# Token operands of an up projection stored tile by tile instead of row by row: one change to a hybrid decoder step

## The chip, the cores and the metric

The kernel runs on one core of one Trainium2 chip. The metric is the device time of one execution, in microseconds (us). Before the change it was 2911.22 us, the median of three runs (2903.2 to 2924.93).

## The reference

One layer of a hybrid decoder is computed, in float32, for a prompt of 2064 tokens (16 learned ones ahead of 2048) and for 8 short sequences of 4 new tokens each: 2096 token rows of width 1024. Attention and a state-space model make an output that is added to the rows. What the change touches is the last part, the feed-forward network:

```
xn2 = rmsnorm(x, norm2)
a, c = xn2 @ w_gate, xn2 @ w_up          # 1024 -> 2816 each
conv = conv_b + sum(conv_w[j] * ap[:, j:j+T] for j in range(3))   # ap: history and a
x = x + (gelu(conv) * c) @ w_down
```

## The kernel before

**Precision.** A float32 product is made of three TensorE products. Each operand is split into a rounded part and a rest: ScalarE (ACT) writes the rounded part, VectorE (DVE) the rest (`split`, lines 67 to 69). `mm3` then issues high by high, high by low and low by high (lines 80 to 82). One split is thus a pair of instructions, one on ACT and one on DVE.

**The up projection** is done by seven products in place of eight (a scheme of Strassen's kind, in Winograd's form). The tokens stand in three blocks of 6, 6 and 5 tiles of 128 rows (`BLOCKS`). In each block, even tiles make one half of the token columns and odd tiles the other, so a block is 3, 3 and 2.2 tiles wide (384, 384 and 280 columns, `width_of`). Each product takes one token operand of 512 features (4 groups `k` of 128) by those columns, and one weight operand. The seven token operands are sums and differences of the quarters of the normed rows. They are made once in `out_norm` (lines 1225 to 1255), in the stage that adds the attention's output projection to the rows: there ACT evicts transposed rows, POOL (GpSimd) forms the differences, and ACT's queue writes each operand to a DRAM scratch array `XB` (helper `keep`, line 1242). `XB` has, for each block, partition and operand, 4 rows (`k`) of 384 columns, so a tile of 128 columns goes out as 4 runs of 512 bytes for each partition and operand.

**Stages in order of time.** Until 1180 us: projections, state-space model, and attention over the prompt, with the output projection of the first six tiles inside it. From about 1200 to 1335 us: `out_attention(range(6, 16), ahead=True)`, the output projection, norm and `XB` writes of ten tiles, with parts of the short sequences' attention (`sample_attention`: gathers of cached keys by indirect DMA, transposes and products on TensorE) put between. From about 1335 to 2425 us: the up projection, 66 units (3 blocks, 11 pairs of feature tiles, gate and up) of 7 products of 12 matmuls, the rest of the short sequences' attention between them. Then the down projection.

**Loads of token operands.** `load_tokens` (lines 1284 to 1299) reads one operand of one block: two loads (`k` 0 and 1, then 2 and 3), each into a raw buffer, each followed by one split of 768 columns a partition (560 in the last block). It is called seven times in `up_setup` for the first block. For each later block it is called right after the last product that used the operand's old contents (`cur["turn"]` in `product`, line 1387): the *turn* of a block, at about 1740 to 1800 us and 2150 to 2195 us. Raw buffers come from pools shared with other work of the stage (tags `raw`, `A`, `z`). The SP queue issues these loads and the weight loads (`load_up`, line 1308) in one order, so a load that waits for its buffer holds up what is behind it.

**Order.** Each engine works through its instructions in a fixed order. The order is made when the program is built, by a planner that simulates a timeline with its own costs (`schedule_with_timeline_sim=True`). ACT's evictions of PSUM (line 1411) and weight splits stand in the same queue as the token splits.

Of the kernel before, what the change touches and what calls it, by code (L numbers as in the profile page):

```python
# [10 lines left out]
F32 = mybir.dt.float32  # L11
# [9 lines left out]
P = 128  # L21
# [25 lines left out]
BLOCKS = [(0, 6), (6, 12), (12, NT)]  # L47
# [3 lines left out]
def width_of(blk):  # L51

    t0, t1 = BLOCKS[blk]
    return (min(t1 * P, T) - t0 * P) // 2


def rows_of(t):
    return P if t < NT - 1 else T - P * (NT - 1)


class Step:
# [81 lines left out]
    def scratch(self, dp):  # L143
        self.KST = dp.tile([H, 2, P, TP], F32, name="KST")
        self.QST = dp.tile([2, H, 2, 64, TP], F32, name="QST")
        self.VST = dp.tile([TP, H * P], F32, name="VST")
        self.VNS = dp.tile([NS * TS, H * P], F32, name="VNS")
        self.UT = dp.tile([512, CH, NU], F32, name="UT")
        self.XNT = dp.tile([12, P, KT, P], F32, name="XNT")
        self.OT = dp.tile([H, P, T], F32, name="OT")  # L150
        self.RR = dp.tile([H, RRW], F32, name="RR")
        self.TBL = dp.tile([2, G, NST, NJ], F32, name="TBL")
        self.GT = dp.tile([CH, 512, NC], F32, name="GT")
        self.ST = dp.tile([2, 4, P, T], F32, name="ST")
        self.X1 = dp.tile([T, D], F32, name="X1")
        self.XB = dp.tile([len(BLOCKS), P, 7, 4, 3 * P], F32, name="XB")
        self.MT = dp.tile([2, P, 11, T], F32, name="MT")

    def load_x(self, xt, t):
# [1065 lines left out]
    def out_norm(self, t, xt, wp, pp):  # L1225
        nc, gp = self.nc, self.nc.gpsimd
        n = rows_of(t)
        xs = self.normed(wp, xt, n, self.g2)
        blk = min(t // 6, 2)
        at = (t - BLOCKS[blk][0]) // 2 * P  # L1230
        last = t == NT - 1
        m = n // 2 if last else P
        if t % 2 == 0:
            self.quarters = [wp.tile([P, 2, 4, P], F32, name="x" + s, tag="x" + s) for s in ("ev", "od")]
        ev, od = self.quarters
        for b in range(2):
            tp = self.half_T(pp, xs, n, b)
            for z, x in enumerate((ev, od)) if last else ((0, (ev, od)[t % 2]),):
                nc.scalar.activation(x[:, b, :, :m], tp[:, :, z * m : z * m + m], AF.Copy)

        def keep(op, x, o=1):
            nc.scalar.dma_start(out=self.XB[blk, :, op : op + o, :, at : at + m], in_=x)

        if t % 2 == 0:
            keep(0, ev[:, :, :, :m], 2)
        if t % 2 or last:
            t1 = wp.tile([P, 2, 4, P], F32, name="xt1", tag="xs")
            keep(2, od[:, 1:2, :, :m])
            gp.tensor_tensor(out=t1[:, 0, :, :m], in0=od[:, 0, :, :m], in1=ev[:, 0, :, :m], op=ALU.subtract)
            gp.tensor_tensor(out=t1[:, 1, :, :m], in0=od[:, 1, :, :m], in1=t1[:, 0, :, :m], op=ALU.subtract)  # L1250
            keep(3, t1[:, :, :, :m], 2)
            gp.tensor_tensor(out=od[:, 0, :, :m], in0=od[:, 1, :, :m], in1=od[:, 0, :, :m], op=ALU.subtract)
            keep(5, od[:, 0:1, :, :m])
            gp.tensor_tensor(out=ev[:, 1, :, :m], in0=ev[:, 1, :, :m], in1=t1[:, 1, :, :m], op=ALU.subtract)
            keep(6, ev[:, 1:2, :, :m])
# [28 lines left out]
    def load_tokens(self, blk, z):  # L1284

        L = width_of(blk)
        op = self.PLACE[z]
        x = self.fx.tile([P, 2, 4, 3 * P], F32R, name="xb", tag=f"xb{op}")
        for k in (0, 2):
            if blk and k == 0:  # L1290
                raw = self.fr.tile([P, 4, 256], F32, name="xraw", tag="raw", bufs=4).rearrange("p k f -> p (k f)")
            else:

                tag = "A" if blk or k else "z"
                raw = self.fz.tile([P, 6 * P + 2 * (tag == "A")], F32, name="xraw", tag=tag, bufs=2)
            raw = raw[:, : 6 * P].rearrange("p (k c) -> p k c", k=2)
            self.nc.sync.dma_start(out=raw[:, :, :L], in_=self.XB[blk, :, op, k : k + 2, :L])
            self.split(x[:, 0, k : k + 2, :L], x[:, 1, k : k + 2, :L], raw[:, :, :L])
        self.xs[z] = x

    def load_up(self, unit):
# [471 lines left out]
```

## Time and profile before

| What | us |
|---|---|
| median of three runs | 2911.22 |
| the profiled execution | 2908.08 |
| its span in the profile | 2906.2 |
| PE (TensorE) busy | 2729.4 |
| DVE busy | 2217.5 |
| ACT busy | 1421.6 |
| POOL busy | 977.4 |

The profile shows one execution. Busy times count instructions of an engine, and the rest of the span is idle time of that engine. Matmul ends are modelled, so a busy PE isn't PE at its peak. Idle time is put down to the instruction or DMA that ended it. The granted clock is the mean share of TensorE's full speed in a stretch, and the DMA share is the mean busy share of the core's 16 DMA engines.

### The profile page before, as it was taken

To read this page: it belongs to the slowest core of one execution; us is meant where nothing else is said; L and a number is where in the kernel's file an instruction comes from. 1 tells how busy PE (TensorE), PEld (TensorE's weight loads), DVE (VectorE), ACT (ScalarE), POOL (GpSimd) and SP (SyncE) were. 2 spreads that over 40 slices of the span, in tenths; PEclk is the share of its full clock that TensorE was granted. 3 is DMA by queue.
4 is the path that set the end of the run, shared out by engine and by line. 5 is a ranking of instruction groups with operands and counts; after the bars stand their busy time and mean duration, and the time that the engine had idled before them with its cause. 6 is when DMAs were issued, how large, how long until landed. Compare 5 with 4: busy or idle time off the path is not lost. (4 is left out here: it accounts for less than half of the span.)

```text
span 2906.2 us, 43491 instructions
## 1 busy us (share of the span) xinstructions
PE 2729.4 (94%) x14872; PEld 2353.4 (81%) x14872; DVE 2217.5 (76%) x4318; ACT 1421.6 (49%) x2887; POOL 977.4 (34%) x1381
## 2 busy tenths in 40 slices
PE   6899889989999999788999999999999999999899
PEld 6866667877887778667998998988998998777776
DVE  6648877767778899558898788888889995674565
ACT  5423334555556666336566556665565663222233
POOL 2525442114444666554243333353213441000000
PEclk9899999999999999989999999999999999999999
DMA  6675676887765342687455546455454447775562
GB/s 180 179 185 142 169 196 178 210 234 202 218 187 157 112 122 85 178 266 233 150 169 180 167 144 211 149 173 161 140 180 133 130 122 270 248 235 186 172 209 87
DMA packets 438135, 512.13 MB, mean 176 GB/s; under 512 B 91338, under 2 KB 339034, under 8 KB 436889
## 3 DMA queue, kind: packets, MB, share of 16 engines
q1 hardware_dynamic: 344440, 361.87, 42.9%
q10 hardware_dynamic: 74576, 79.09, 8.1%
q0 software_dynamic: 18896, 68.39, 7.5%
q8 instruction: 117, 1.92, 0.3%
q14 instruction: 106, 0.86, 0.1%
HBM read 381.32 MB, written 126.74 MB: 175 GB/s over the span
## 5 line engine op out<-in xcount | busy, mean ns | idle before, releaser
L80 PE MATMUL g<-xb,uw 128*128 128x384 f32 (+1 forms) x1848 | 596.0, 325 | 10.5 <-ACT uw L68 4.1
L81 PE MATMUL g<-xb,uw 128*128 128x384 f32 (+1 forms) x1848 | 595.1, 323 | 1.1 <-DVE xb L69 1.1
L82 PE MATMUL g<-xb,uw 128*128 128x384 f32 (+1 forms) x1848 | 583.5, 323 | 0.9 <-DVE uw L69 0.9
L80 PEld LDWEIGHTS g<-xb,uw 128*128 128x128 f32 x1848 | 347.5, 188 | 23.3 <-ACT uw L68 5.2
L81 PEld LDWEIGHTS g<-xb,uw 128*128 128x128 f32 x1848 | 347.9, 188 | 8.9 <-issue 2.3
L82 PEld LDWEIGHTS g<-xb,uw 128*128 128x128 f32 x1848 | 344.8, 188 | 7.9 <-DVE uw L69 1.8
L491 ACT ACTIVATE p<-S,nms 128x484 f32<-128x484 f32 (+11 forms) x360 | 210.5, 592 | 144.3 <-DVE nms L490 125.0
L69 DVE TENSOR_TENSOR uw<-uraw,uw 128x512 fp32r<-128x512 f32 x330 | 241.7, 739 | 25.3 <-ACT uw L68 23.5
L68 ACT ACTIVATE uw<-uraw 128x512 fp32r<-128x512 f32 x330 | 200.4, 625 | 113.8 <-PE g L82 70.5
L80 PE MATMUL pq<-dw,da 128*128 128x512 f32 x528 | 208.3, 396 | 15.0 <-DVE dO L1601 8.4
L490 DVE TENSOR_REDUCE nms<-S 128x1 f32<-128x484 f32 (+11 forms) x360 | 190.2, 554 | 31.8 <-PE S L485 23.1
L81 PE MATMUL pq<-dw,da 128*128 128x512 f32 x528 | 207.9, 394 | 0.0
L82 PE MATMUL pq<-dw,da 128*128 128x512 f32 x528 | 200.5, 394 | 3.1 <-DVE da L69 3.1
L80 PE MATMUL pj<-wh,x 128*128 128x512 f32 (+1 forms) x408 | 169.1, 417 | 14.9 <-DVE wk L337 5.9
L95 POOL TENSOR_TENSOR rs_y<-rs_v,half 128x8 f32<-128x8 f32 (+4 forms) x77 | 95.6, 1247 | 252.7 <-DVE rs_v L90 230.8
L68 ACT ACTIVATE da<-dt 128x1024 fp32r<-128x1024 f32 (+1 forms) x68 | 71.0, 1046 | 210.8 <-PE pq L82 133.0
L81 PE MATMUL pj<-wl,x 128*128 128x512 f32 (+1 forms) x408 | 168.7, 413 | 3.5 <-DVE wl L75 3.5
L1323 POOL TENSOR_TENSOR uraw<-uraw 128x512 f32<-128x512 f32 x66 | 111.0, 1682 | 171.0 <-DVE s L1321 124.4
L82 PE MATMUL pj<-wh,x 128*128 128x512 f32 (+1 forms) x408 | 167.6, 412 | 0.0
L484 PE MATMUL S<-kt,qs 128*128 128x484 f32 (+11 forms) x360 | 144.9, 405 | 13.6 <-ACT p L491 7.3
L521 POOL TENSOR_TENSOR p<-p,g 128x412 f32<-128x412 f32 (+13 forms) x164 | 155.7, 977 | 3.7
L553 PE MATMUL O<-wT,vt 128*128 128x256 f32 x576 | 143.6, 386 | 8.9 <-DVE wT L550 7.4
(432 smaller groups left out, 6930.4 us busy)
## 6 DMA issues: line engine op xcount, KB each, us to landing
dt<-MT SPq DMA_DIRECT2D x99, 512.0 KB
uraw<-in_w_gate_dram SPq DMA_DIRECT2D x66, 512.0 KB
uraw<-in_w_up_dram SPq DMA_DIRECT2D x66, 512.0 KB
raw<-in_w_in_dram SPq DMA_DIRECT2D x80, 256.0 KB
MT<-z ACTq DMA_DIRECT2D x44, 384.0 KB
qs<-QST SPq DMA_DIRECT2D x128, 128.0 KB
draw<-in_w_down_dram SPq DMA_DIRECT2D x55, 256.0 KB
dT<-in_w_down_dram SPq DMA_DIRECT2D x55, 256.0 KB
```

The costliest lines, as they stand in the source:

```text
L68: nc.scalar.activation(hi, src, AF.Copy)
L69: nc.vector.tensor_tensor(out=lo, in0=src, in1=hi.bitcast(F32), op=ALU.subtract)
L80: mm(out, lhsT=lh, rhs=rh, start=start, stop=False, skip_group_check=goes_on)
L81: mm(out, lhsT=lh, rhs=rl, start=False, stop=False, skip_group_check=goes_on)
L82: mm(out, lhsT=ll, rhs=rh, start=False, stop=stop, skip_group_check=goes_on)
L95: nc.gpsimd.tensor_tensor(out=y, in0=v, in1=e, op=ALU.pow)
L484: nc.tensor.matmul(dst, lhsT=qs[:, 0, c, qa : qa + M], rhs=kt[c][:, x:y], start=True, stop=False)
L490: nc.vector.tensor_reduce(out=nms[:M, z : z + 1], in_=dst, axis=AX.X, op=ALU.max, negate=True)
L491: nc.scalar.activation(p[:M, Z + x : Z + y], dst, AF.Exp, bias=nms[:M, z : z + 1], accum_out=sms[:M, z : z + 1])
L521: nc.gpsimd.tensor_tensor(out=pw[1][:M, x], in0=pw[1][:M, x], in1=g[:M, z : z + 1].to_broadcast([M, x.stop - x.start]), op=ALU.mult)
L553: nc.tensor.matmul(O[:, :N], lhsT=v, rhs=tw[:, m - a, :N], start=(m == 0), stop=(m == nb))
L1323: gp.tensor_tensor(out=a21, in0=a11, in1=a21, op=ALU.subtract)
```

## The change

`XB` is laid out as block, partition, operand, then column tile, then `k`, then 128 columns. One tile of one operand is then 2 KB in one piece for each partition. Writes of the last tile, which is 24 columns wide in each half, are issued operand by operand. A load takes two pieces of a tile and a half (3 KB a partition each) where the columns are full. In the last block, the second piece is one load of 1 KB a partition and one of 4 runs of 24 columns. Each piece is split by two pairs of instructions: tile 0 whole (512 columns) and `k` 0 and 1 of tile 1 (256), then `k` 2 and 3 of tile 1 (256) and tile 2 whole (512, in the last block 96).

```diff
-        self.XB = dp.tile([len(BLOCKS), P, 7, 4, 3 * P], F32, name="XB")
+        self.XB = dp.tile([len(BLOCKS), P, 7, 3, 4, P], F32, name="XB")
...
-        at = (t - BLOCKS[blk][0]) // 2 * P
+        at = (t - BLOCKS[blk][0]) // 2
...
         def keep(op, x, o=1):
-            nc.scalar.dma_start(out=self.XB[blk, :, op : op + o, :, at : at + m], in_=x)
+
+            for z in range(o) if last else [slice(0, o)]:
+                to = self.XB[blk, :, op + z, at, :, :m] if last else self.XB[blk, :, op : op + o, at]
+                nc.scalar.dma_start(out=to, in_=x[:, z])
...
-        for k in (0, 2):
-            if blk and k == 0:
+        kept = self.XB[blk, :, op].rearrange("p j k c -> p (j k c)")
+        n = L - 2 * P
+        for half in range(2):
+            if blk and half == 0:
                 raw = self.fr.tile([P, 4, 256], F32, name="xraw", tag="raw", bufs=4).rearrange("p k f -> p (k f)")
             else:
-                tag = "A" if blk or k else "z"
+                tag = "A" if blk or half else "z"
                 raw = self.fz.tile([P, 6 * P + 2 * (tag == "A")], F32, name="xraw", tag=tag, bufs=2)
-            raw = raw[:, : 6 * P].rearrange("p (k c) -> p k c", k=2)
-            self.nc.sync.dma_start(out=raw[:, :, :L], in_=self.XB[blk, :, op, k : k + 2, :L])
-            self.split(x[:, 0, k : k + 2, :L], x[:, 1, k : k + 2, :L], raw[:, :, :L])
+            a = 6 * P * half
+            if half == 0 or n == P:
+                self.nc.sync.dma_start(out=raw[:, : 6 * P], in_=kept[:, a : a + 6 * P])
+            else:
+                self.nc.sync.dma_start(out=raw[:, : 2 * P], in_=kept[:, a : a + 2 * P])
+                self.nc.sync.dma_start(out=raw[:, 2 * P : 6 * P].rearrange("p (k c) -> p k c", c=P)[:, :, :n],
+                                       in_=self.XB[blk, :, op, 2, :, :n])
+            for j, k0, k1, at in ((1, 2, 4, 0), (2, 0, 4, 2 * P)) if half else ((0, 0, 4, 0), (1, 0, 2, 4 * P)):
+                w = n if j == 2 else P
+                src = raw[:, at : at + (k1 - k0) * P].rearrange("p (k c) -> p k c", c=P)[:, :, :w]
+                self.split(x[:, 0, k0:k1, j * P : j * P + w], x[:, 1, k0:k1, j * P : j * P + w], src)
```

## Rows read from the trace of the kernel before

**Rows 1.** The page: the span, and the engines' busy time, share and instructions.

```profile
span 2906.2 us, 43491 instructions
...
PE 2729.4 (94%) x14872; PEld 2353.4 (81%) x14872; DVE 2217.5 (76%) x4318; ACT 1421.6 (49%) x2887; POOL 977.4 (34%) x1381
```

**Rows 2.** Windows: stretch, length, busy us by engine, clock, DMA share, GB/s.

```profile
1220.00:1260.00 40.00, 35.74 (x174) 29.64 (x174) 22.64 (x42) 14.78 (x28) 23.99 (x21) 0.91 0.91 268
1260.00:1300.00 40.00, 34.41 (x173) 29.11 (x174) 21.70 (x36) 14.81 (x28) 25.45 (x23) 0.91 0.87 275
1300.00:1340.00 40.00, 27.61 (x135) 21.79 (x134) 26.09 (x40) 18.88 (x33) 17.12 (x17) 0.87 0.87 277
...
1460.00:1760.00 300.00, 299.93 (x1690) 272.81 (x1689) 249.60 (x367) 174.20 (x290) 111.55 (x119) 1.00 0.52 161
1760.00:1800.00 40.00, 37.33 (x216) 34.84 (x214) 33.78 (x49) 25.57 (x43) 8.03 (x9) 1.00 0.80 264
...
2160.00:2200.00 40.00, 35.19 (x221) 33.79 (x219) 34.30 (x56) 23.21 (x42) 7.07 (x11) 0.96 0.55 166
...
2240.00:2420.00 180.00, 179.39 (x1393) 177.99 (x1392) 173.96 (x375) 110.88 (x218) 74.16 (x100) 1.00 0.41 122
```

**Rows 3.** What PE waited for, 1180 to 1345 us: total us, times, longest.

```profile
PE tp L188 <- DVE xs L180: 11.1, 4, 4.8
PE tps L648 <- DMA kv<-in_cache_k_dram,idx: 10.5, 6, 3.2
PE tpr L580 <- DVE rs_y L99: 5.9, 1, 5.9
...
PE Sp L654 <- DVE kT L69: 0.5, 2, 0.2
```

**Rows 4.** ACT's DMA queue, 1173 to 1186 us: packets, MB, share of 16 engines.

```profile
q10 hardware_dynamic: 2624, 1.31, 36.1%
```

**Rows 5.** The same queue, 1380 to 1460 us.

```profile
q10 hardware_dynamic: 576, 1.57, 4.9%
```

**Rows 6.** The same queue, 2100 to 2112 us.

```profile
q10 hardware_dynamic: 3722, 0.47, 28.8%
```

**Rows 7.** Splits on ACT by tile, whole span: ns min/median/max, first and last start, forms.

```profile
L68 ACT ACTIVATE uw<-uraw x330: 609/624/661, 1334.1 to 2416.8; 128x512 fp32r<-128x512 f32 x165
...
L68 ACT ACTIVATE xb<-xraw x42: 657/833/856, 1328.5 to 2193.2; 128x768 fp32r<-128x768 f32 x28, 128x560 fp32r<-128x560 f32 x14
...
L68 ACT ACTIVATE gh<-gT x32: 401/406/488, 499.7 to 610.2; 128x256 fp32r<-128x256 f32 x28, 128x336 fp32r<-128x336 f32 x4
```

**Rows 8.** Splits on DVE by tile, whole span, the same columns.

```profile
L69 DVE TENSOR_TENSOR uw<-uraw,uw x330: 670/682/2175, 1335.7 to 2418.4; 128x512 fp32r<-128x512 f32 x165
...
L69 DVE TENSOR_TENSOR xb<-xraw,xb x42: 728/946/1829, 1329.4 to 2193.9; 128x768 fp32r<-128x768 f32 x28, 128x560 fp32r<-128x560 f32 x14
...
L69 DVE TENSOR_TENSOR gl<-gT,gh x32: 405/420/509, 500.2 to 612.0; 128x256 fp32r<-128x256 f32 x28, 128x336 fp32r<-128x336 f32 x4
```

**Rows 9.** What PE waited for, 1735 to 1840 us, the first turn.

```profile
PE g L80 <- ACT c L1411: 2.0, 2, 1.3
PE g L80 <- DVE A L1420: 1.2, 1, 1.2
```

**Rows 10.** ACT in order, 1779 to 1785 us: start, us, instruction, idle before and releaser.

```profile
1781.19 0.84 ACT L68 ACTIVATE xb<-xraw 128x768 fp32r<-128x768 f32 x1 [4.94 <-DMA xraw<-XB]
1781.94 0.47 ACT L1411 ACTIVATE c<-g 128x384 f32<-128x384 f32 x1
```

**Rows 11.** What PE waited for, 2145 to 2250 us, the second turn.

```profile
PE g L80 <- ACT uw L68: 4.1, 3, 2.9
```

**Rows 12.** What PE waited for, 1325 to 1400 us, the first block's start.

```profile
PE g L81 <- DVE xb L69: 1.1, 1, 1.1
...
PE g L80 <- ACT xb L68: 0.6, 1, 0.6
```

**Rows 13.** SP's issues of token loads, whole span: ns min/median/max, first and last start.

```profile
L1297 SPq DMA_DIRECT2D xraw<-XB x42: 319/339/500, 1195.9 to 2190.3; - x42
```

## The prediction

> **What bounds the kernel now.** I read the page first: TensorE (PE) is busy for 2729.4 of 2906.2 us [rows 1]. A change off PE can win at most the rest, and only where PE waits for what the change touches. So the next view is the table by windows [rows 2]. In the up projection's steady stretch PE is busy for 299.93 of 300 us: nothing is to be won there. Three places are different. The stretch of the attention's output projection, where the operands are written, has PE busy for 97.8 of 120 us (1220 to 1340), a granted clock of 0.91, 0.91 and 0.87, and a DMA share of 0.91, 0.87 and 0.87: the DMA engines are nearly full. The windows at the two turns, where operands are loaded, have PE busy for 37.33 and 35.19 of 40 us. Last, the views of what PE waited for in these places: gathers and normed rows in the first [rows 3], ACT's evictions and weight splits and a DVE instruction at the turns [rows 9, 11], the token splits themselves at the first block's start, for 1.7 us [rows 12].
>
> **Part 1: runs of 2 KB where there were four of 512 bytes.** The price of a run is read from windows in which ACT's queue carries one kind of transfer. At 1173 to 1186 us it moves `XB` writes alone: 0.361 x 16 x 13 us = 75.1 us for 2624 packets, 28.6 ns for 512 bytes [rows 4]. At 1380 to 1460 us it moves rows of 3 KB of the products' results: 0.049 x 16 x 80 = 62.7 us, and 1.57 MB are 512 such packets (the rest are tiny), 122 ns each [rows 5]. A line through the two gives 84 ns at 2 KB, an estimate. Four runs of 512 bytes take 114 ns, so 30 ns in 114 go away. A pair of tiles writes 7 operands x 128 partitions x 4 runs = 3584 packets. The ten tiles of the stretch are five pairs: 17,920 packets x 28.6 ns / 16 engines = 32.0 us of all engines before, 4480 x 84 / 16 = 23.5 us after. **8.5 us of DMA time are freed**, some 0.07 of the share over 120 us.
>
> What PE gets of it: at least nothing, since PE is itself busy for 81% of the stretch. At most all 8.5 us, if DMA sets the pace, and with it what the lowered clock costs: busy time times missing clock, 35.74 x 0.09 + 34.41 x 0.09 + 27.61 x 0.13 = 9.9 us [rows 2]. That is 18.4 us. I see no way in which larger packets lose time here: the bytes and the issues for full tiles stay the same. Between the ends I go by the row that is a direct wait for DMA, the gathers' 10.5 us, against 11.1 us for normed rows behind DVE [rows 3]. Together with the eight smaller waits of that view, 5.9 us down to 0.5 us and 15.9 us in all, they make 37.5 us, so 28% of PE's waiting is for DMA: 0.28 x 8.5 = **2.4 us gained**.
>
> By the Trainium skill (DMA: Bandwidth & Descriptors, section Specifications) transfers of 512 bytes and more already run at line rate; by it this part would give nothing and the term would be 0. The rows say otherwise, 512 bytes in 28.6 ns against 3 KB in 122, 17.9 bytes a ns against 25.2 [rows 4, 5].
>
> **Part 2: four pairs of splits where there were two.** A full operand was 2 x 833 ns on ACT and 2 x 946 on DVE. Now it is two splits of 512 columns and two of 256: 2 x 624 + 2 x 406 = 2060 ns on ACT, 2 x 682 + 2 x 420 = 2204 on DVE, so +0.39 and +0.31 us [rows 7, 8]. In the last block it was two of 560 (the minima, 657 and 728 ns), and is 512, 256, 256 and 96. For 96 columns I go down the line from 512 over 256, which gives 0.27 us on ACT and 0.26 on DVE (estimates): +0.39 and +0.32 us. Seven operands cost **+2.8 us of ACT and +2.2 us of DVE** at the start and at each turn. The two engines are not full there (33.78 of 40 us on DVE at the first turn, 34.30 at the second), so most is covered. What isn't covered goes through the order of ACT. The rows at 1781 us show it: a token split waits 4.94 us for its load, the eviction of a product's PSUM bank stands behind it [rows 10], and PE waits for that eviction. Three such waits make 3.2 us at the first turn, three weight splits 4.1 us at the second [rows 9, 11]. Lower end 0: nothing in the chain gets shorter, so no gain. Upper end: all of both engines' extra time in series, 5.0 us a turn. I take one operand's extra ACT time for each of three waits, as those rows are nearest: 3 x 0.39 = **1.2 us for each turn**.
>
> **Part 3: what a product waits for.** Before, its first six matmuls needed `k` 0 and 1, that is the first load only. Now the first matmul runs over all columns and needs all four pairs. At the turns no row shows PE waiting for a token split, so this stays hidden as long as the loads come more than a product ahead; if that cover goes, it costs half a product each. At the first block's start PE does wait, 1.7 us [rows 12]. It gets longer by 0, if the splits are there anyway, up to the seven operands' ACT and DVE time, 5.0 us. I take the excess of two operands on one engine, some **1 us**, as only two such waits are seen.
>
> **Part 4: loads and issues.** In the first two blocks a load stays one run of 3 KB a partition. In the last block an operand was 512 runs of 1120 bytes, by the line above 51 ns each: 1.6 us of 16 engines. It becomes 128 of 3 KB, 128 of 1 KB (47 ns) and 512 of 96 bytes. The packets of 1 x 96 bytes, as the last tile writes them, took at most 0.288 x 16 x 12 / 3722 = 14.9 ns [rows 6]. That is 1.8 us, +0.2 us an operand, at a DMA share of 0.55. SP gets seven more issues of 0.34 us [rows 13], 2.4 us in all. Behind each stand the next token or weight loads. They wait for buffers that DVE frees, so the extra issues lie beside that: 0, and 2.4 us if the cover goes. ACT gets two more issues for the last tile; they stand ahead of block 3 by tens of us, and cost 0.
>
> **The sum**, against the profiled execution's 2908.08 us (a span of 2906.2, and 1.9 around it; the median of the three runs is 3.1 above it): -2.4 + 2 x 1.2 + 1 = +1.0, **2909 us**: no change.
>
> **Rivals.**
> *DMA sets the pace of the output projection.* For it: a share of 0.87 to 0.91 and the clock. Against: PE's largest wait there is not a DMA. All 18.4 us come back, less 3.4 of parts 2 and 3: 2893 us. Chance 0.13.
> *The turns become the bound (slower).* The place is ACT's and DVE's queue at 1760 to 1800 and 2160 to 2200 us: evictions and weight splits behind token splits that wait for their loads, whose raw buffers are freed by two pairs instead of one. It decides as soon as the extra time is not absorbed between two loads. For it: PE's waits at both turns already have that form [rows 9 to 11], and DVE has 173.96 of 180 us filled after the second turn [rows 2], so that what is late there stays late. Against: 5 to 6 us of idle DVE time in each window. Price: 2 x 5.0 + 2.4 for SP's issues + 1 to 5 at the start, less 2.4: 2919 to 2923 us. Chance 0.18.
> *The planner orders it differently.* Durations of the writes and the splits enter its simulation, so the order of the output projection and of the short sequences' attention can change, with either sign. The room is PE's 22 us of idle time and 10 us of clock in 1220 to 1340: 2890 to 2930 us, and further in few cases. Chance 0.14.
> *The writes gain nothing,* because 512 bytes are enough for the engines (the section named above says so, the trace does not) or because the new pieces still go out in 512 bytes: 2908.08 + 3.4 = 2911.5 us. Against the second: the loads of two full `k` rows are already merged into one run. Chance 0.10.
>
> **How the numbers follow.** The forecast keeps 0.45: 2909 us, by itself 2903 to 2915. The range takes in the first rival at 2893, a little below for the planner, and the slower one, with the before's own spread of 2903 to 2925 in mind: **2889 to 2926**. A difference of 1%, 29 us, is about what a measurement of this kernel can tell from no change. Faster by more needs nearly all of PE's idle time in the stretch plus the clock: 0.01 from the first rival and 0.05 from the planner, 0.06. Slower by more: 0.05 from the planner and 0.01 from the turns, 0.06. Within 1%: 0.88.
>
> **What the profile after would show.** ACT's queue in the output projection with a quarter of the packets, near 84 ns each, and a DMA share some 0.07 lower in 1220 to 1340; the gathers' share of PE's waits smaller; 84 token splits on each engine with the durations above; PE's busy time at the turns within 1 to 2 us of before. Wrong would be: a stretch shorter by 10 us or more (DMA did set the pace), PE waiting for token splits at the turns (part 3 uncovered), or the up projection starting much earlier or later with the same waits (the order).

## The result, and the profile after

The changed kernel takes 2928.9 us (median of 14 runs, 2917.73 to 2941.26). The kernel before, run beside it, takes 2915.16 us (14 runs), 3.9 us above the median of three and 7.1 us above the one execution from which the prediction's sum started (2908.08). The ratio is **1.0054** (95% interval 1.0039 to 1.0068): slower by half a per cent, some 16 us by the ratio and 13.7 us between the medians. Forecast were 2909 us and no change, with a range that ended at 2926. The prediction held 1% to be about the least that can be told; the interval here is 0.15% to either side.

The page after, its span and its engines (answers to [rows 1]):

```profile
span 2932.0 us, 43579 instructions
...
PE 2737.6 (93%) x14872; PEld 2364.4 (81%) x14872; DVE 2221.3 (76%) x4360; ACT 1422.9 (49%) x2929; POOL 983.6 (34%) x1381
```

The profiled execution is 25.8 us longer (a second one of each kernel: 2923.3 against 2901.7, 21.6 us). PE's busy time grows by 8.2 us, with the same 14,872 matmuls and a lower mean granted clock, 0.974 against 0.978. That the clock is the whole of it isn't shown: `c2` below has 2744.2 us of busy time at 0.976. The other 17.6 us are idle time of PE, 194.4 against 176.8. ACT and DVE have 42 instructions more each, as forecast, and only 1.3 and 3.8 us more to do.

The windows after (answer to [rows 2]; columns as there):

```profile
1220.00:1260.00 40.00, 33.87 (x165) 28.78 (x166) 23.15 (x37) 15.12 (x28) 23.00 (x22) 0.91 0.82 254
1260.00:1300.00 40.00, 34.12 (x175) 28.45 (x174) 22.04 (x40) 15.31 (x28) 22.40 (x22) 0.96 0.81 280
1300.00:1340.00 40.00, 26.94 (x120) 21.10 (x118) 23.20 (x38) 16.62 (x32) 15.22 (x15) 0.79 0.73 249
...
1760.00:1800.00 40.00, 37.43 (x212) 35.72 (x211) 35.76 (x62) 27.92 (x57) 11.73 (x10) 0.96 0.66 213
2160.00:2200.00 40.00, 33.21 (x200) 32.40 (x198) 30.92 (x59) 21.50 (x47) 5.10 (x6) 0.97 0.59 164
```

The DMA share of the output projection fell by 0.09, 0.06 and 0.14, as it should with larger packets. Over all 20 profiles of this case, the share of 1220 to 1340 us is 0.83 to 0.88 with the old layout (ten) and 0.76 to 0.79 with the new one (ten). PE got nothing of it: it is busy for 94.9 us of the 120, after 97.8, and the up projection's first product starts at 1340.0 us, after 1335.0 (second executions: 1338.5 after 1333.2). The second turn lost 2 us of PE, the first none.

What PE waited for at 1180 to 1345 us (answers to [rows 3]):

```profile
PE tp L188 <- DVE xs L180: 14.5, 5, 3.5
PE tps L648 <- DMA kv<-in_cache_k_dram,idx: 11.3, 5, 4.6
PE tpr L580 <- DVE rs_y L99: 5.9, 1, 5.9
```

The gathers still cost 11.3 us (10.5 before), with DMA engines that are freer. One number of each would not settle it, as second executions of the same two programs have 8.9 and 12.5 us. But over the 20 profiles the wait is 10.3 to 13.5 us with the old layout and 8.9 to 15.3 us with the new one: it doesn't follow the fullness of the engines.

ACT's queue at 1173 to 1187 us, where it carries `XB` writes (answers to [rows 4]; packets, MB, share of 16 engines):

```profile
q10 hardware_dynamic: 704, 1.31, 25.0%
```

The same 1.31 MB took 0.25 x 16 x 14 = 56.0 us of DMA time after 75.1 us: at most 87.5 ns for each of 640 packets of 2 KB, where 84 had been estimated. The Trainium skill (DMA: Bandwidth & Descriptors, section Specifications) has transfers of 512 bytes and more at line rate; the price of a packet here says otherwise, 17.9 bytes a ns at 512 bytes and 23.4 at 2 KB, but no time came of the difference (`g2` below).

The token splits on ACT and on DVE (answers to [rows 7, 8]):

```profile
L68 ACT ACTIVATE xb<-xraw x84: 266/418/652, 1333.6 to 2208.4; 128x256 fp32r<-128x256 f32 x42, 128x512 fp32r<-128x512 f32 x35, 128x96 fp32r<-128x96 f32 x7
```

```profile
L69 DVE TENSOR_TENSOR xb<-xraw,xb x84: 244/422/1762, 1334.3 to 2209.4; 128x256 fp32r<-128x256 f32 x42, 128x512 fp32r<-128x512 f32 x35, 128x96 fp32r<-128x96 f32 x7
```

Their number and their durations are those of the forecast (for 96 columns 266 and 244 ns against 270 and 260).

Three waits are new or longer. PE's waits at the start of the first block (1325 to 1410 us, answers to [rows 12]), at the second turn (2145 to 2260 us, answers to [rows 11]), and at the change from the up to the down projection (2415 to 2600 us), all after:

```profile
PE g L80 <- ACT xb L68: 3.9, 1, 3.9
...
PE g L80 <- ACT uw L68: 6.4, 2, 5.5
PE g L81 <- DVE xb L69: 1.1, 1, 1.1
...
PE pq L80 <- ACT da L68: 4.3, 2, 2.6
PE pq L80 <- DVE z L1443: 2.8, 1, 2.8
PE pq L82 <- DVE da L69: 1.5, 1, 1.5
```

The last group in the kernel before:

```profile
PE pq L80 <- ACT da L68: 1.7, 1, 1.7
PE pq L82 <- DVE da L69: 1.1, 1, 1.1
```

The last place is the surprise. The change edits nothing there and moves no data of it, yet PE waits 8.6 us in place of 2.8, and the clock falls behind the waits (windows around the change to the down projection, which stands at 2443.7 us after and 2425.6 before; first after, then before; columns as in [rows 2]):

```profile
2420.00:2440.00 20.00, 19.90 (x157) 19.62 (x156) 17.80 (x43) 10.75 (x22) 6.74 (x11) 1.00 0.36 126
2440.00:2460.00 20.00, 14.60 (x61) 11.57 (x60) 5.68 (x14) 4.77 (x6) 2.61 (x4) 0.91 0.61 199
```

```profile
2420.00:2440.00 20.00, 19.28 (x100) 16.26 (x99) 8.47 (x21) 4.90 (x6) 2.87 (x5) 1.00 0.75 246
2440.00:2460.00 20.00, 20.00 (x88) 16.34 (x88) 6.50 (x8) 5.88 (x8) 0.00 (x0) 1.00 1.04 399
```

What stands differently there is one group of PE's instructions: the four short transposes (tile `tpe`) with which the convolution's last columns are written out. After, PE issues them one product (12 matmuls) ahead of the down projection; before, two products ahead. Rows of PE and of DVE around the change, first after, then before:

```profile
2438.50 0.49 PE L1485 MATMUL tpe<-ident,hs 128*128 128x128 f32 x3
...
2442.40 0.29 DVE L1487 COPY ends<-tpe 96x128 f32<-96x128 f32 x1 [1.09 <-DMA out_dram<-ends]
...
2443.03 0.50 DVE L1443 TENSOR_TENSOR z<-g,z 128x256 f32<-128x256 f32 x2
```

```profile
2420.98 0.49 PE L1471 MATMUL tpe<-ident,hs 128*128 128x128 f32 x3
...
2424.74 0.29 DVE L1473 COPY ends<-tpe 96x128 f32<-96x128 f32 x1 [0.80 <-DMA out_dram<-ends]
...
2425.63 0.40 PE L80 MATMUL pq<-dw,da 128*128 128x512 f32 x1
...
2425.83 0.52 DVE L1429 TENSOR_TENSOR z<-g,z 128x256 f32<-128x256 f32 x2 [0.38 <-PE g L82]
```

In both, DVE's last copy out of `tpe` waits for a DMA, and its last work on the up projection (`z<-g`) stands behind that copy. After, the first matmul of the down projection waits for this work and starts at 2443.68, though PE's last product was done at 2440.9. Before, it doesn't wait for it: it starts at 2425.63, ahead of it.

### The profile page after: what moved, and what is told of

Same layout as the page of the kernel before. It is cut to its first block, busy times and chain, and to the rows that moved or that the text cites. A ratio compares the mean times of both kernels' runs of the same rounds, so it can differ in the third digit from the quotient of the medians.

```text
span 2932.0 us, 43579 instructions
## 1 busy us (share of the span) xinstructions
PE 2737.6 (93%) x14872; PEld 2364.4 (81%) x14872; DVE 2221.3 (76%) x4360; ACT 1422.9 (49%) x2929; POOL 983.6 (34%) x1381
```

## The experiments

Two theories. **Work**: the added instructions (four pairs of splits, SP's issues) or the new layout cost by themselves. **Order**: the planner, which simulates the whole program with its own costs, writes another order of instructions for every engine, and that order is better or worse in places far from the edit. The first expectations say theory one for the added instructions, theory two for the order and theory three for the new layout's transfers. All ratios are to the kernel before, run on the same chip, with 95% intervals.

**The parts, and a control that changes next to no work.**

`e1_split4`: four pairs on the old layout and loads.

```diff
-            self.split(x[:, 0, k : k + 2, :L], x[:, 1, k : k + 2, :L], raw[:, :, :L])
+            for c in (slice(0, 2 * P), slice(2 * P, L)):
+                self.split(x[:, 0, k : k + 2, c], x[:, 1, k : k + 2, c], raw[:, :, c])
```

> The kernel before, with its layout, writes and loads, but each piece split by two pairs of instructions (512 and 256 columns; in the last block 512 and 48). If the added splits are what costs (theory one), the ratio to the kernel before is 1.003 to 1.006, with the up projection's start and the two turns together 5 to 12 us longer. If the planner's new order costs whatever the work is (theory two), the ratio lies anywhere from 0.996 to 1.006 and the lost time is not at the start and the turns. If the new layout's transfers cost (theory three), it is 0.999 to 1.001.

Measured: 2915.47 us, 1.0007 (0.9990 to 1.0025). Four pairs alone, on the old layout, don't make the loss.

`e2_after_two_pairs`: the changed kernel, with one pair of 768 columns for each piece in the first two blocks (the columns land in other places than they should; the work is what is compared).

```diff
-            for j, k0, k1, at in ((1, 2, 4, 0), (2, 0, 4, 2 * P)) if half else ((0, 0, 4, 0), (1, 0, 2, 4 * P)):
+            if n == P:
+                src = raw[:, : 6 * P].rearrange("p (k c) -> p k c", k=2)
+                self.split(x[:, 0, 2 * half : 2 * half + 2], x[:, 1, 2 * half : 2 * half + 2], src)
...
```

> The changed kernel with its layout, writes and loads, but in the first two blocks each piece is split by one pair of 768 columns, straight through, so that the token columns land in another place than they should (the numbers are not the reference's; the amount of work is that of the kernel before). Theory one: back to 0.999 to 1.002, with the first product and the first turn as before. Theory two: anywhere from 0.996 to 1.006. Theory three: stays at 1.004 to 1.006.

Measured: 2921.44 us, 1.0024 (1.0005 to 1.0043). Under half of the loss stays, with an interval almost as wide as the loss.

`e3_k_pairs`: the new layout and its 2 KB writes, but loads of two `k` in three runs of 1 KB, each with one pair of splits (in the last block, each in two loads and two pairs). The lines that go are those of the kernel before.

```diff
-            raw = raw[:, : 6 * P].rearrange("p (k c) -> p k c", k=2)
-            self.nc.sync.dma_start(out=raw[:, :, :L], in_=self.XB[blk, :, op, k : k + 2, :L])
-            self.split(x[:, 0, k : k + 2, :L], x[:, 1, k : k + 2, :L], raw[:, :, :L])
+            raw = raw[:, : 6 * P].rearrange("p (j k c) -> p j k c", j=3, k=2)
+            for j, j1, w in ((0, 3, P),) if n == P else ((0, 2, P), (2, 3, n)):
+                self.nc.sync.dma_start(out=raw[:, j:j1, :, :w], in_=self.XB[blk, :, op, j:j1, k : k + 2, :w])
+                hi, lo = [x[:, s, k : k + 2, j * P : j * P + (j1 - j) * w].rearrange("p k (j c) -> p j k c", c=w) for s in range(2)]
+                self.split(hi, lo, raw[:, j:j1, :, :w])
```

> The changed kernel's layout and 2 KB writes, but loads of two k rows over all tiles (three runs of 1 KB in place of one of 3 KB), each split by one pair of 768 columns (in the last block by a pair of 512 and one of 48), so that a product's first six matmuls need the first load alone, as in the kernel before. Theory one, with what a product waits for counted in: 0.998 to 1.002. Theory two: anywhere from 0.996 to 1.006. Theory three, by the writes: 1.003 or more; by the longer loads alone: 0.999 to 1.001.

Measured: 2919.57 us, 1.0022 (1.0006 to 1.0038), as e2.

`c1_pool_memset`: the kernel before, with a one-column memset on POOL after each of the 21 operand loads.

```diff
+        self.nc.gpsimd.memset(self.ones[:, 0:1], 1.0)
         self.xs[z] = x
```

> The kernel before with one added memset of a single column on POOL for each load of an operand, 21 in all, that changes no number and next to no work, but changes the planner's order. Theory one and theory three: 0.999 to 1.001. Theory two: the ratio differs from 1 by 0.002 to 0.006, with either sign.

Measured: 2917.25 us, 1.0017 (1.0003 to 1.0031). Twenty-one instructions that do next to nothing cost about what a part of the change does, in an interval that just leaves out 1. They don't run where they are written: in the trace all stand on POOL at 1194 to 1216 us, 98 ns each, the first behind a wait of 0.8 us for PE. From here on, order was a theory that had to be controlled for.

**What the first matmul waits for, and the changed kernel in another order.**

`f1_k_last_first` (the kernel before, each product's `k` in the order 2, 3, 0, 1, so that its first matmul needs the second load) and `f2_split4_k_last_first` (the same with four pairs):

```diff
-            for k in range(4):
+            for k in (2, 3, 0, 1):
...
```

> The kernel before, its layout, loads and two pairs of splits, but each product of the up projection takes the k groups in the order 2, 3, 0, 1, so that its first matmul needs the second load of its token operand, as in the changed kernel. If waiting for the later load is what the changed kernel pays for (theory one), the ratio is 1.002 to 1.004, lost at the start and the turns. If the planner's order is (theory two), it lies where the memset control lies, 0.998 to 1.003. The rival that neither counts: 1.000.

> The kernel before with its layout and loads, with four pairs of splits (512, 256, 512, 256 columns) and with the k groups in the order 2, 3, 0, 1: more splits and a first matmul that needs the last of them, without the new layout's transfers. Theory one: 1.003 to 1.006, as the changed kernel. Theory two: 0.998 to 1.004, no more than the control. If the transfers are needed for the loss (theory three): 1.000 to 1.002.

Measured: 1.0007 (0.9991 to 1.0023) and 1.0019 (1.0001 to 1.0036). A product that waits for its operand's later load costs nothing that stands out, though up to 0.23% (f1) and 0.36% (f2, with four pairs) stay possible.

`f3_after_pool_memset`: the changed kernel with the 21 memsets on POOL.

> The changed kernel with one added memset of a single column on POOL for each load of an operand, next to no work but another order from the planner. Theory one and three: 1.004 to 1.007 against the kernel before, as without it. Theory two: it moves from 1.0054 by 0.002 or more, with either sign.

Measured: 2925.38 us, 1.0040 (1.0021 to 1.0060). 21 instructions more, and it isn't slower than the changed kernel (1.0054); the move of 0.002 that theory two asked for didn't come. PE's waits at the change to the down projection are back at the size of before (1.7 and 1.1 us): PE is busy for 20.00 of 20 us at 2440 to 2460, across the change (here at 2441.0), at full clock, and the transposes stand two products ahead again.

`b2_before_again`, a single execution of the kernel before:

> The kernel before once more, for a second profile of the same program: how far the stages' lengths differ between two executions of one program. All theories: within 0.5% of the median, stage by stage within some 8 us.

Measured: 2903.57 us, with a span of 2901.7. Two profiles of one program differ by 4.5 us here.

**The last block's pieces.**

`g1_compact`: the changed kernel, with the 24 columns of the last tile's four `k` stored side by side. The second piece is then one load of 1408 bytes a partition; SP's seven extra issues and the runs of 96 bytes are gone.

```diff
...
-            if half == 0 or n == P:
-                self.nc.sync.dma_start(out=raw[:, : 6 * P], in_=kept[:, a : a + 6 * P])
-            else:
-                self.nc.sync.dma_start(out=raw[:, : 2 * P], in_=kept[:, a : a + 2 * P])
-                self.nc.sync.dma_start(out=raw[:, 2 * P : 6 * P].rearrange("p (k c) -> p k c", c=P)[:, :, :n],
-                                       in_=self.XB[blk, :, op, 2, :, :n])
+            N = 6 * P if half == 0 else 2 * P + 4 * n
+            self.nc.sync.dma_start(out=raw[:, :N], in_=kept[:, a : a + N])
...
```

> The changed kernel, but the last tile's 24 columns are stored side by side (4 x 24 in one piece behind tile 1), so that in the last block too an operand is loaded by two issues of one run each (3 KB and 1408 bytes), without the seven extra issues and the 3584 runs of 96 bytes. If SP's queue at the second turn (weight loads behind more token loads) is part of the loss, PE's idle time in the second turn goes from 9 back to about 6 us and the ratio from 1.0054 to 1.003 to 1.0045. If the splits or the order alone are the cause: 1.0045 to 1.0065, the second turn as in the changed kernel.

Measured: 2927.0 us, 1.0043 (1.0027 to 1.0059).

`g2_compact_two_pairs`: g1 with the two pairs of e2.

> The same, and in the first two blocks one pair of splits of 768 columns a piece, straight through, so that the token columns there land in another place than they should (the amount of work is that of the kernel before). What is left of the change is its writes, its layout, and the last block's four pairs. If splits and extra issues are the loss: 0.999 to 1.001. If the planner's order is: 1.001 to 1.003, as the controls. If the new layout itself costs: 1.003 or more.

Measured: 2916.79 us, **1.0000** (0.9985 to 1.0014). The new layout, its 2 KB writes and its loads in 3 KB pieces cost and bring nothing that can be told from zero, to some 4 us. PE's waits at the second turn, first in g1, then in g2:

```profile
PE g L80 <- DVE A L1432: 3.9, 1, 3.9
...
PE g L80 <- ACT uw L68: 0.4, 1, 0.4
```

```profile
PE g L80 <- DVE A L1436: 3.7, 1, 3.7
...
PE g L80 <- ACT uw L68: 0.6, 1, 0.6
```

The waits of PE for ACT's weight splits of 6.4 us in all, which the changed kernel has (e2: 6.2 us, f3: 4.6 us), are under 1 us without the extra loads. A shorter one for DVE stands in their place.

`c2_dve_memset`: the kernel before with the memsets on DVE. `a2_after_again`: a single execution of the changed kernel.

> A second control: the kernel before with one memset of a single column on DVE for each load of an operand, 21 in all, some 0.1 us each. If any other order of the planner costs, 1.001 to 1.003 as with the first control; if the first control's loss was chance, 0.999 to 1.001.

> The changed kernel once more, for a second profile. The stages that the change reaches (output projection to the end of the up projection) are as long as in its first profile within 4 us in all; the down projection, whose code is untouched, is 446 us as in every other profile, and not 457 as in the first.

Measured: 2925.77 us, 1.0030 (1.0013 to 1.0046), for the first; 2925.09 us, with a span of 2923.3, for the second. An order can cost 0.3%: these 21 memsets are 59 ns each, 1.2 us in all, and stand at 48 to 75 us, far from the loads behind which they are written. The up projection starts at 1345.9 us there (1335.0 and 1333.2 in the kernel before). And the changed kernel's waits at the down projection come back with the program: 4.3, 2.9 and 1.4 us, against the expectation, by which its down projection would be as short as in every other profile. From the first matmul of the down projection to the end of the span, the changed kernel takes 488.3 us and, the second time, 485.1 us; g1, which has the same waits, 482.1 us; the other 17 profiles 476.6 to 480.8 us.

**Four and two pairs under other orders.** The memsets were added to the changed kernel on DVE (`h1`), to g1 (`h2`), g2 (`h3`) and e1 (`h4`) on POOL.

> The changed kernel with a one-column memset on DVE after each of its 21 operand loads: no work to speak of (21 x under 0.1 us), but another written order. Theory 'the planner's order carries the loss': the ratio to before falls anywhere between 1.000 and 1.005, and it is small where PE's wait for the `da` split and for `z` at the change from up to down projection (4.3 + 2.8 us in the changed kernel) is absent. Theory 'four pairs of splits on the new layout cost by themselves': 1.004 to 1.006, with or without that wait.

> The changed kernel with the last tile stored side by side (one load for the second piece in every block), and a one-column memset on POOL after each operand load: four pairs, no extra SP issues, another order. Theory 'order': between 1.000 and 1.004, decided by the change from up to down projection (PE waits of some 5 us there or none). Theory 'four pairs on the new layout cost by themselves': 1.0035 to 1.006, as without the memsets (1.0043).

> The same with one pair of 768 columns for each piece in the first two blocks (columns land in other places: the output is not the reference's) and the memsets on POOL. Theory 'order': between 1.000 and 1.004, no better on the mean than the version with four pairs. Theory 'four pairs on the new layout cost by themselves': 0.999 to 1.002, at least 0.2% under the version with four pairs and the same memsets.

> The kernel before with four pairs of splits per operand on its own layout and loads, and the memsets on POOL. Theory 'order': between 1.000 and 1.004, as the memsets alone (1.0017). Theory 'four pairs cost only on the new layout': as the memsets alone, 1.000 to 1.003. If four pairs cost in either layout but were offset by a lucky order in the first trial (1.0007): 1.003 to 1.005.

Measured: 1.0061 (1.0040 to 1.0082), 1.0019 (0.9997 to 1.0042), 1.0030 (1.0014 to 1.0045) and 0.9995 (0.9974 to 1.0016). With these memsets two pairs are no better than four (h3 against h2), and four pairs on the old layout are as fast as the kernel before. That speaks against four pairs as a fixed price. g1 and h2 differ by the memsets alone, and with them by the place of the transposes. PE's waits at the change to the down projection, first in g1, then in h2:

```profile
PE pq L80 <- ACT da L68: 4.3, 2, 2.6
PE pq L80 <- DVE z L1441: 2.7, 1, 2.7
PE pq L82 <- DVE da L69: 1.2, 1, 1.2
```

```profile
PE pq L80 <- ACT da L68: 1.7, 1, 1.7
PE pq L82 <- DVE da L69: 1.6, 1, 1.6
```

h1, though, is as slow as the changed kernel without those waits (1.7 and 1.1 us there), against its expectation, so they are not the whole of it: another order can lose in another place. h1's up projection starts at 1353.7 us, the changed kernel's at 1340.0.

**The added instructions on the old layout.** `i1_last_block_issues` issues the second load of each operand of the last block as two; `i2_last_block_issues_split4` adds the four pairs.

```diff
-            self.nc.sync.dma_start(out=raw[:, :, :L], in_=self.XB[blk, :, op, k : k + 2, :L])
+            if blk == 2 and k:
+                for i in range(2):
+                    self.nc.sync.dma_start(out=raw[:, i, :L], in_=self.XB[blk, :, op, k + i, :L])
+            else:
+                self.nc.sync.dma_start(out=raw[:, :, :L], in_=self.XB[blk, :, op, k : k + 2, :L])
```

> The kernel before, with the second load of each operand in the last block issued as two loads (k 2 and k 3 apart): the 7 extra SP issues of the change in the last block, on the old layout, loads and splits. Theory 'the extra issues cost': PE waits 7 to 9.5 us in the second turn (5.9 in the kernel before) and the ratio is 1.001 to 1.002. Theory 'only the order the planner makes counts': between 0.9995 and 1.003, with the second turn as before.

> The same with four pairs of splits per operand: all instructions that the change adds (splits and SP issues), on the old layout. Theory 'the added instructions cost by themselves': 1.003 to 1.005, near the changed kernel (1.0040 to 1.0061 in three orders). Theory 'order': between 0.9995 and 1.003, since the old layout leaves the planner's other choices as they were.

Measured: 0.9990 (0.9970 to 1.0010) and 1.0000 (0.9984 to 1.0016). The splits and SP's issues that the change adds, on the old layout, cost nothing that can be told from zero (0.16%, some 5 us).

### What the runs say together

Each program has a fixed list of instructions for PE, 14,474 of them as built (the trace, which counts another way, has 14,872 matmuls). Told apart by operation, tile names and sizes, these lists are the same, place by place, in the kernel before, i1, g2 and e2; in the changed kernel and g1; in c1 and h3; and in f3 and h2. (Which slice of a tile is read still differs in places, 15 between the changed kernel and g1, 243 and 268 between the kernel before and g2 or e2, 728 and 593 in the last two pairs.) Between the kernel before and the changed one, 750 places hold another instruction (matmuls that stand earlier or later), and ACT's and DVE's lists differ more. So the ratios can be read along these lines:

| comparison | differences of ratios, in % |
|---|---|
| last block's pieces with the extra load and runs of 96 bytes, against side by side; PE's list the same | after - g1 +0.11, f3 - h2 +0.21, e2 - g2 +0.24 |
| four pairs against two; PE's list changes with it | after - e2 +0.30, g1 - g2 +0.43, h2 - h3 -0.11, e1 - before +0.07, h4 - c1 -0.22, f2 - f1 +0.12, i2 - i1 +0.10 |
| layout, writes and loads (side by side) against the old; PE's list the same | g2 - before 0.00, h3 - c1 +0.13 |
| memsets: another order, and 1 to 2 us of work on DVE or POOL | c1 +0.17, c2 +0.30, f3 - after -0.14, h1 - after +0.07, h2 - g1 -0.24, h3 - g2 +0.30, h4 - e1 -0.12 |

By the intervals of the two ratios, a difference is good to 0.14 to 0.30% to either side. Clear of zero are c1, c2, h3 - g2, after - e2 and g1 - g2.

The last row is the yardstick: an order that has next to nothing to do with the work costs up to 0.3%; that one gains is not shown, as the three negative values are within their intervals. Against that, four pairs come to +0.10% on the mean of seven (2.9 us), with both signs; the extra load of the last block to +0.19% on the mean of three (5.4 us), always of one sign, though each of the three is within its intervals; the layout to 0.07% (1.9 us). These make 0.36% of the 0.54%, and 0.18%, 5 us, remain.

Step by step from the kernel before, the way is shorter: g2 stands at 0.00, the step to g1 is +0.43 and the one to the changed kernel +0.11. So most of the loss comes with four pairs in place of two in the first two blocks. But under the memsets the same step, h3 to h2, is -0.11. The two are 0.54 apart, where their four intervals together leave some 0.35 (an estimate from the recorded intervals): the step has no fixed price, it depends on the order that comes with it.

One place of that order is found. Of the 18 programs only the changed kernel and g1 have the four `tpe` transposes one product ahead of the down projection, and only they have the long waits there. The memsets alone move the transposes and take the waits away (f3 and h2). In the traces the down projection of these two is longer than the mean of the other 17 profiles, 479.2 us, by 9.1 and 5.9 us in the changed kernel and by 2.9 us in g1. What the place is worth in the time of the whole is not measured apart: f3 - after and h2 - g1 have the sign, -0.14 and -0.24, but are within their intervals. And in f3, at 1.0040 without the waits, the rest of the loss isn't located.

## Why the prediction was wrong

**The order, which the sum left out.** The step that failed is the one that wasn't in the sum at all: the terms took the kernel's order as given, and "the planner orders it differently" stood beside as a rival with a chance of 0.14, its room placed in the output projection. The runs put the order's effect at up to 0.3%, 9 us, for edits that do next to no work, and its largest single trace here at 2440 us, 8.6 us of waits in place of 2.8: over 1000 us behind the output projection's writes and 236 us behind the start of the last token load. The profile of before couldn't name that place. Of the signs that the prediction gave for this rival, a later start of the up projection came, by 5 us.

**Part 1, 2.4 us gained: wrong.** The packets and their price came out as forecast (87.5 ns against 84), and the DMA share fell by 0.06 to 0.14 against the 0.07 worked out. But g2, which has all of it, two pairs in the first two blocks and PE's list of before, is at 1.0000 (0.9985 to 1.0014). The 28% share of DMA in PE's waits was the wrong measure: over the 20 profiles the gathers' wait doesn't fall with freer engines. The rival that the writes gain nothing was right about this term, though not for the reason given, and not about the time; DMA as the pace of the stretch, worth 18.4 us, is excluded by g2.

**Part 2, 1.2 us a turn, and part 3, 1 us: not contradicted.** Together they made 3.4 us; seven comparisons of four pairs with two give 2.9 us on the mean, but from -6 to +13 us one by one, so that the nearness is luck. The way given for part 2 isn't seen: its three waits at the first turn (one of which, 1.2 us for DVE's `A`, wasn't behind ACT at all [rows 9]) are gone after, and no new wait for token splits stands there. The start shows one of 3.9 us where 1.7 stood: there part 3, 1 us, came out as 2.2. That a product waits for its later load costs nothing that stands out (f1).

**Part 4, nothing: probably wrong for the last block.** The prediction named 2.4 us if SP's cover goes. At the second turn it went. SP in order at 2189 to 2196 us after (start, us, instruction), then the ACT rows and the PE row of what waited:

```profile
2190.60 0.38 SPq L1322 DMA_DIRECT2D uraw<-in_w_up_dram  x1
2191.11 0.43 SPq L1306 DMA_DIRECT2D xraw<-XB  x1
2191.59 0.43 SPq L1307 DMA_DIRECT2D xraw<-XB  x1
2194.25 0.37 SPq L1322 DMA_DIRECT2D uraw<-in_w_up_dram  x1
```

```profile
2196.29 0.42 ACT L68 ACTIVATE xb<-xraw 128x256 fp32r<-128x256 f32 x1 [2.34 <-DMA xraw<-XB]
...
2199.46 1.15 ACT L68 ACTIVATE uw<-uraw 128x512 fp32r<-128x512 f32 x2 [2.17 <-DMA uraw<-in_w_up_dram]
```

```profile
2200.15 0.60 PE L80 MATMUL g<-xb,uw 128*128 128x280 f32 x1 [5.51 <-ACT uw L68]
```

Weight loads stand between and behind the token loads, at 2190.60 and 2194.25. ACT and PE have to wait for one of them until 2199.46 (the profile doesn't say which), and PE waits 5.51 us for its split. In [rows 11] the longest such wait is 2.9 us. The issues alone don't make the loss: i1 has the same seven, 5.5 us of such waits in all where [rows 11] have 4.1, and a time no longer than before. Whether it is the 512 runs of 96 bytes of each of those loads, or what stands around them, wasn't separated. Nor do the waits at this turn account for all of the 5.4 us: all of PE's waits there together are 9.4 us in the changed kernel and 6.5 in g1, 9.3 in e2 and 7.6 in g2, 7.2 in f3 and 6.7 in h2.

**The rival of the turns** was slower for a reason that the runs speak against: i2 has its extra splits and issues and stands at 1.0000 (0.9984 to 1.0016), on the old layout, where the rival asked for 11 to 15 us. The measured time of 2928.9 us lies 3 us above the range, and 20 us above the forecast. 7 us of the 20 are the starting point, one execution of the kernel before (2908.08) that lay below its median over more runs (2915.16); the rest is the change, 13.7 us between the medians where 1.0 had been worked out.

## What to carry to other kernels

Where a planner writes the order, an edit is two changes: its work, and a new draw of the order everywhere. Before a few tenths of a per cent are put down to the work, add an instruction that does next to nothing and see what that costs, and look up in the trace where the planner put it; and give "another order" a chance and a width in the forecast that such controls support. DMA time that is freed is worth time only where a wait is shown to end with bandwidth, not merely with a DMA.

## What was not expected of the hardware

The gathers' wait did not fall with the DMA share of its stretch: 10.3 to 13.5 us at 0.83 to 0.88, 8.9 to 15.3 us at 0.76 to 0.79, ten profiles each. And a short stall can be paid for twice. PE's first matmuls of the down projection in the changed kernel, in order (start, us):

```profile
2443.68 0.76 PE L80 MATMUL pq<-dw,da 128*128 128x512 f32 x1 [2.79 <-DVE z L1443]
2444.25 0.63 PE L81 MATMUL pq<-dw,da 128*128 128x512 f32 x1
...
2447.05 0.40 PE L82 MATMUL pq<-dw,da 128*128 128x512 f32 x1
```

Behind 2.79 us of waiting a matmul takes 0.63 us, and 3 us later 0.40 us. The granted clock of 2440 to 2460 us is 0.91, a mean over the two levels of 1.2 and 2.4 GHz; in the second execution, 0.98 and 0.93 in the two windows. But not each time: g1 has the same stall, 2.69 us, and behind it the same matmuls take 0.47 and then 0.40 us, at a granted clock of 1.00 from 2440 to 2500 us. Why one execution pays and the other doesn't stays open.
